# Decoder trunk on one core: side work pauses for eight steps ahead of each wide up-projection group

## The chip, the cores and the metric

The kernel runs on one core of a Trainium2 chip. The metric is the device time of one execution in microseconds; three runs of the kernel before took 2248.45, 2249.08 and 2250.85 us (median 2249.08 us). The profile is of one further execution on the same kind of core.

## What is computed

Two decoder layers over 256 positions of width 2048, in float32. Each layer is a mixer (layer 0: a Mamba-2 scan beside block attention; layer 1: a three-branch sparse attention beside retention), then a convolutional feed-forward network, each followed by a scaled residual and a layer norm. The change lies in the feed-forward part:

```python
D_MODEL, SEQ, DEPTH, FFN_DIM, FFN_CONV = 2048, 256, 2, 5632, 3

def conv_ffn(x, w_up, conv_w, conv_b, w_down):
    a, u = jnp.split(x @ w_up, 2, axis=-1)
    a = causal_depthwise_conv(a, conv_w, conv_b)
    return (jax.nn.silu(a) * u) @ w_down

for layer in range(DEPTH):
    ...
    h = layer_norm(DEEPNORM_ALPHA * h + mix, ln_g[layer, 0], ln_b[layer, 0])
    ffn = conv_ffn(h, ffn_w_up[layer], ffn_conv_w[layer], ffn_conv_b[layer], ffn_w_down[layer])
    h = layer_norm(DEEPNORM_ALPHA * h + ffn, ln_g[layer, 1], ln_b[layer, 1])
```

## The kernel before

**Matmuls.** Every float32 operand is held as a high and a low part, and each product is three matmuls (high by high, high by low, low by high). Weights come from HBM in slabs of mostly 128x1024 numbers (L185, issued by SP into six buffers `wraw`); ScalarE copies out the high part `whi` (L210), VectorE subtracts to get the low part `wlo` (L218), four buffers each. `get` looks three slabs ahead of TensorE.

**Seven products for eight.** Some pairs of 128-row blocks are multiplied with seven block products in place of eight (letters R and N in `PLAN`; P is a plain pair). For these, sums of weight blocks are needed. N forms them when the slabs arrive (`add_up`, L229, into `other` or `sums`). R reads them from DRAM, where they were kept earlier: that is the **side work** of the change. One **cycle** of it (`make`, L231) is two loads of 512 KB into the tile `sums` (L240, issued by POOL), four adds of 128x512 on VectorE (L246), and two stores of 512 KB to DRAM tiles `sumdown...` (L250, POOL). In layer 1 there are 15 cycles for the down projection, all in the one tile `sums`, so a load waits until the stores ahead of it have landed, and the adds wait for the load. `sum_up` (L499) makes the like sums of activations, with VectorE (L509, L513) and a split into high and low parts (L337 on ScalarE, L338 on VectorE).

**The feed-forward part** (`ffn`, L1633) computes the up projection in groups of 256 columns, `a` and `u` in turn (`group_b`, L387: 16 blocks of 128 rows, 64 matmuls), and at a few places one **wide group** of 1024 columns (`group_m`, L517, plan NPNPNPNP): at j=7 in layer 0, at j=4, 8 and 12 in layer 1 (`WIDE_UP`). The last `group_b` ahead of a wide group at j is the one for `u` of j-1 (i odd in the loop). The evacuation of each group multiplies and splits the result into `g` and, from a certain column on, `high`, the input of the down projection.

**Order of the side work.** `Fill` is a list of steps, some of them empty. `group_b` takes one step every second block, so eight in a group. A wide group takes its steps from another list (`aux`) and puts six empty steps ahead of the first when it is done. A cycle of layer 1 spans 14 steps: load, wait 5, add, 1, store, 5 (`CYCLES`, `cycles`). Whatever is left after the last group is run at once (`flush`, L1728). When the last up group of layer 1 starts, the list holds 4 steps, fewer than the eight that the group takes. The emitted instructions then go through a scheduler which sets each engine's order; each engine runs its own in that order.

**Start of the down projection, layer 1.** `finish_rows` (L886) makes four rows for the end of the kernel. It clears `sums` on VectorE (L913), loads rows of `lnrow` into it (L914, by SP), and works them with `rows` on ScalarE (L918, L920) and VectorE (L919, L921), using blocks 0 to 3 of `x` as room. `sum_up` puts the activation sums of the first R pairs into those same blocks of `x`. The first group of the down projection is a `group_m` with the plan PPPPRPRP...: four plain pairs (96 matmuls) come ahead of the first R pair, whose second product reads the first sums in `x`.

Of the kernel before, what the change touches and what calls it, by code (L numbers as in the profile page):

```python
# [321 lines left out]
class Trunk:  # L322
# [1310 lines left out]
    def ffn(self, layer):  # L1633
        nc, x = self.nc, self.x
        with ExitStack() as ctx:
            P = ctx.enter_context(self.tc.tile_pool(name="ffn", bufs=1))
            up, early = ExitStack(), ExitStack()
            wide, first = WIDE_UP[layer], FIRST[layer]
# [57 lines left out]
            def inner(j0):  # L1696
                def turn(j, own, evac):
                    ps = self.ps()
                    for o in range(2):
                        for t in range(2):  # L1700
                            c = 256 * (j - j0) + 128 * o
                            nc.tensor.transpose(ps[:, 256 * o + 128 * t:256 * o + 128 * t + 128], own[t][:, c:c + 128],
                                                self.ident)
                    evac(ps.rearrange("p (a b) -> p a b", a=2), False)

                def go(z):
                    for j in (j0, j0 + 1):
                        for n, f in enumerate((ev_a, ev_u)):
                            self.aux.add(1, lambda j=j, n=n, f=f: turn(j, [z[t][n] for t in range(2)], f(j)))
                return go  # L1710
# [3 lines left out]
            for i, e in enumerate(evacs[3:], 3):  # L1714
                j = i // 2
                if 2 * j == first and i % 2 == 0:
                    assert not self.aux.q and not (double and left)
                    early.close()
                    high = ctx.enter_context(self.tc.tile_pool(name="high", bufs=1)).tile([128, FT - first, 512], F32R, name="high")
                    g = Parts(low, high)  # L1720
                    at = lambda k: g[:, k:k + 2, :]
                if j in wide and i % 2 == 0:
                    assert not self.aux.q
                    self.group_m(x, f"up{layer}", wide.index(j), 0, inner=inner(j))
                    self.fill.q[:0] = [lambda: None] * 6
                elif j not in wide and j - 1 not in wide:
                    self.group_b(x, [e])
            self.fill.flush()  # L1728
            up.close()
# [139 lines left out]
```

## Time and profile before

| what | us |
|---|---|
| runs, median of 3 (lowest to highest) | 2249.08 (2248.45 to 2250.85) |
| the profiled execution: its span, first to last instruction | 2246.8 |
| median of the runs above that span | 2.3 |
| TensorE busy in it | 2235.3 |
| VectorE busy in it | 1831.3 |
| ScalarE busy in it | 1254.0 |
| matmul `ps` at L539 waiting for ScalarE's `whi`, two times | 2.7 |

The span runs from the first to the last instruction of the profiled execution; what a timed run has beyond it lies ahead of and behind the instructions. PE is TensorE, PEld its weight load, DVE is VectorE, ACT is ScalarE, POOL is GpSimd, SP issues most DMAs; a q behind an engine is its sequencer. A row of a timeline gives the start, the duration, the engine, the line and operation, what is written from what, the shape, and in brackets the idle time before it and what ended it. `x2` is a merge of two alike instructions.

### The profile page before, as it was taken

To read this page: it belongs to the slowest core of one execution; us is meant where nothing else is said; L and a number is where in the kernel's file an instruction comes from. 1 tells how busy PE (TensorE), PEld (TensorE's weight loads), DVE (VectorE), ACT (ScalarE), POOL (GpSimd) and SP (SyncE) were. 2 spreads that over 40 slices of the span, in tenths; PEclk is the share of its full clock that TensorE was granted. 3 is DMA by queue.
4 is the path that set the end of the run, shared out by engine and by line. 5 is a ranking of instruction groups with operands and counts; after the bars stand their busy time and mean duration, and the time that the engine had idled before them with its cause. 6 is when DMAs were issued, how large, how long until landed. Compare 5 with 4: busy or idle time off the path is not lost.

```text
span 2246.8 us, 32995 instructions
## 1 busy us (share of the span) xinstructions
PE 2235.3 (99%) x12125; PEld 1920.9 (85%) x12125; DVE 1831.3 (82%) x2795; ACT 1254.0 (56%) x1718; POOL 126.4 (6%) x219
## 2 busy tenths in 40 slices
PE   9999999999999999999999999999999999999998
PEld 9888888888888888888898888888888888888887
DVE  5788688988877778887977777889988887779887
ACT  5555555655555556656645564457555565557563
POOL 0101000110011100000000000000100001100000
PEclk9999999999999999999999999999999999999999
DMA  9854456897788886888668534467876768888884
GB/s 312 292 175 161 158 194 189 274 376 264 238 302 302 296 284 213 292 286 274 211 208 287 188 114 154 152 209 235 290 227 228 255 217 297 300 273 276 276 280 169
DMA packets 158780, 546.33 MB, mean 243 GB/s; under 512 B 17827, under 2 KB 19283, under 8 KB 158483
## 3 DMA queue, kind: packets, MB, share of 16 engines
q1 hardware_dynamic: 132937, 451.41, 60.1%
q0 software_dynamic: 25536, 92.55, 11.8%
q8 instruction: 95, 1.56, 0.3%
q14 instruction: 68, 0.56, 0.1%
q10 hardware_dynamic: 144, 0.26, 0.0%
HBM read 502.19 MB, written 41.96 MB: 242 GB/s over the span
## 4 chain that ended last, share of the span: by engine, by line
PE 96%; DVE 2%; issue 1%; ACT 0%; POOL 0%; DMA 0%; SPq 0%; ACTq 0%; POOLq 0%; DVEq 0%
PE acc L427 51%; PE ps L540 7%; PE ps L541 7%; PE ps L539 7%; PE acc L627 3%; PE acc L629 3%; PE acc L628 3%; PE acc L540 3%; PE acc L541 3%; PE acc L539 3%; PE ps L628 1%; PE ps L627 1%; PE ps L629 1%; PE ps L1161 1%; PE ps L427 1%
## 5 line engine op out<-in xcount | busy, mean ns | idle before, releaser
L210 ACT ACTIVATE whi<-wraw 128x1024 fp32r<-128x1024 f32 (+4 forms) x882 | 875.1, 1002 | 549.6 <-PE acc L427 219.0
L218 DVE TENSOR_TENSOR wlo<-wraw,whi 128x1024 fp32r<-128x1024 f32 (+4 forms) x882 | 1007.5, 1153 | 209.6 <-ACT whi L210 197.6
L427 PE MATMUL acc<-x,whi 128*128 128x512 f32 x3296 | 1032.2, 398 | 0.0
L427 PEld LDWEIGHTS acc<-x,wlo 128*128 128x128 f32 x3296 | 604.0, 188 | 136.5 <-DVE wlo L218 0.3
L427 PE MATMUL acc<-x,wlo 128*128 128x256 f32 x3296 | 633.8, 279 | 0.0
L427 PEld LDWEIGHTS acc<-x,whi 128*128 128x128 f32 x3296 | 510.0, 189 | 9.7 <-issue 1.1
L689 ACT ACTIVATE tmp<-acc 128x512 f32<-128x512 f32 x104 | 62.2, 598 | 167.8 <-PE acc L427 167.7
L246 DVE TENSOR_TENSOR sums<-sums 128x512 f32<-128x512 f32 x140 | 96.2, 687 | 10.5 <-DMA sums<-in_down 9.4
L540 PE MATMUL ps<-wlo,g 128*128 128x512 f32 x260 | 101.3, 390 | 0.0
L541 PE MATMUL ps<-whi,g 128*128 128x512 f32 x260 | 101.2, 389 | 0.0
L539 PE MATMUL ps<-whi,g 128*128 128x512 f32 x260 | 101.2, 389 | 0.0
L539 PE MATMUL ps<-whi,x 128*128 128x512 f32 x244 | 94.0, 390 | 2.7 <-ACT whi L210 2.7
L540 PE MATMUL ps<-wlo,x 128*128 128x512 f32 x244 | 95.5, 391 | 0.1
L541 PE MATMUL ps<-whi,x 128*128 128x512 f32 x244 | 95.0, 389 | 0.0
L627 PE MATMUL acc<-whi,x 128*128 128x344 f32 (+3 forms) x224 | 74.9, 336 | 0.7 <-ACT whi L210 0.7
L628 PE MATMUL acc<-wlo,x 128*128 128x344 f32 (+3 forms) x224 | 74.5, 333 | 0.3 <-DVE wlo L218 0.3
L629 PE MATMUL acc<-whi,x 128*128 128x344 f32 (+3 forms) x224 | 74.3, 332 | 0.0
L1681 DVE SCALAR_TENSOR_TENSOR c<-fpad,prm,c 128x256 f32<-128x256 f32 x176 | 74.2, 479 | 0.0
L210 ACT ACTIVATE whi<-other 128x1024 fp32r<-128x1024 f32 x32 | 33.7, 1055 | 57.7 <-DVE other L229 56.9
L250 POOL DMA_DIRECT2D sumdown<-sums x62 | 33.3, 537 | 570.9 <-DVE sums L246 570.8
L540 PEld LDWEIGHTS ps<-wlo,g 128*128 128x128 f32 x260 | 48.8, 188 | 10.5 <-DVE wlo L218 0.4
L539 PEld LDWEIGHTS ps<-whi,g 128*128 128x128 f32 x260 | 48.8, 188 | 10.3
(458 smaller groups left out, 3141.6 us busy)
## 6 DMA issues: line engine op xcount, KB each, us to landing
wraw<-in_up SPq DMA_DIRECT2D x328, 512.0 KB, 4.8
wraw<-in_down SPq DMA_DIRECT2D x142, 512.0 KB, 4.8
wraw<-in_od_in SPq DMA_DIRECT2D x96, 512.0 KB, 4.2
wraw<-in_ev_in SPq DMA_DIRECT2D x72, 512.0 KB, 4.1
wraw<-sumdown SPq DMA_DIRECT2D x68, 512.0 KB, 4.5
sums<-in_down POOLq DMA_DIRECT2D x62, 512.0 KB, 6.8
sumdown<-sums POOLq DMA_DIRECT2D x62, 512.0 KB, 5.4
wraw<-in_ev_out SPq DMA_DIRECT2D x30, 512.0 KB, 3.9
```

What stands on the lines that cost most here:

```text
L210: a = nc.scalar.activation(hi[:, :n], raw[:, :n], AF.Copy)
L218: b = nc.vector.tensor_tensor(lo[:, :n], raw[:, :n], hi[:, :n].bitcast(F32), op=OP.subtract)
L246: self.tc.keep_in_program_order(nc.vector.tensor_tensor(o, x, y, op=OP.add))
L427: nc.tensor.matmul(acc, wt, mv, start=(k == 0 and i < len(unit)), stop=(k == nk - 1 and i >= len(unit)))
L539: nc.tensor.matmul(o, xh, wh, start=n not in used, stop=False)
L540: nc.tensor.matmul(o, xh, wl, start=False, stop=False)
L541: nc.tensor.matmul(o, xl, wh, start=False, stop=stop)
L627: nc.tensor.matmul(o, xh, wh, start=start, stop=False)
L628: nc.tensor.matmul(o, xh, wl, start=False, stop=False)
L629: nc.tensor.matmul(o, xl, wh, start=False, stop=stop)
L689: nc.scalar.activation(t, a[:, :, 256:], AF.Copy, scale=sign)
L1681: nc.vector.scalar_tensor_tensor(c[:, i, :], pad[:, i, t:t + 256], w[:, t:t + 1], c[:, i, :], op0=OP.mult, op1=OP.add)
```

## The change

In the loop of `ffn`, ahead of the `u` group that stands directly before a wide group, eight empty steps are put at the front of the list. That is the whole group's share, so no step of the side work is taken in it; all later steps come eight steps later. This happens once in layer 0 (j=6) and three times in layer 1 (j=3, 7, 11).

```diff
                 elif j not in wide and j - 1 not in wide:
+                    if j + 1 in wide and i % 2:
+                        self.fill.q[:0] = [lambda: None] * 8
                     self.group_b(x, [e])
             self.fill.flush()
             up.close()
```

No instruction is added or removed. In layer 1 the list is 24 steps longer by the end, so 28 steps are there when the last group starts, and 20 are left to `flush`: the last adds and stores of the second last cycle, and the load, adds and stores of the last. `order` below means the place of instructions on an engine in the built program.

First place, VectorE, the wide group of layer 0 (j=7), from the split of the group ahead of it. `other` holds sums of weight blocks made by `add_up`. Before:

```order
L338 TENSOR_TENSOR g<-u,g 128x2x256
L246 TENSOR_TENSOR sums<-sums 128x512
L218 TENSOR_TENSOR wlo<-wraw,whi 128x1024
L246 TENSOR_TENSOR sums<-sums 128x512
L218 TENSOR_TENSOR wlo<-wraw,whi 128x1024
L246 TENSOR_TENSOR sums<-sums 128x512
L229 TENSOR_TENSOR other<-wraw 128x512
L246 TENSOR_TENSOR sums<-sums 128x512
L229 TENSOR_TENSOR other<-other,wraw 128x512
L229 TENSOR_TENSOR other<-wraw 128x512
L229 TENSOR_TENSOR other<-other,wraw 128x512
```

Now:

```order
L338 TENSOR_TENSOR g<-u,g 128x2x256
L218 TENSOR_TENSOR wlo<-wraw,whi 128x1024 x2
L229 TENSOR_TENSOR other<-wraw 128x512 x2
L229 TENSOR_TENSOR other<-other,wraw 128x512
L218 TENSOR_TENSOR wlo<-wraw,whi 128x1024
L229 TENSOR_TENSOR other<-other,wraw 128x512
L218 TENSOR_TENSOR wlo<-other,whi 128x1024
```

The four adds of a cycle (L246) are gone from here; they stand behind the wide group's evacuation. The wide group at j=4 of layer 1 shows the same.

Second place, VectorE, the wide group at j=12 of layer 1. `fpad` and `u` are the evacuations of the two groups ahead of it. Before:

```order
L246 TENSOR_TENSOR sums<-sums 128x512
L229 TENSOR_TENSOR other<-other,wraw 128x512
L246 TENSOR_TENSOR sums<-sums 128x512
L218 TENSOR_TENSOR wlo<-wraw,whi 128x1024
L246 TENSOR_TENSOR sums<-sums 128x512
L229 TENSOR_TENSOR other<-other,wraw 128x512
L246 TENSOR_TENSOR sums<-sums 128x512
L692 TENSOR_TENSOR fpad_14545<-acc,tmp 128x2x256
L218 TENSOR_TENSOR wlo<-wraw,whi 128x1024
L1681 SCALAR_TENSOR_TENSOR c<-fpad_14545,prm,c 128x256 x4
L229 TENSOR_TENSOR other<-wraw 128x512
```

Now:

```order
L692 TENSOR_TENSOR fpad_14545<-acc,tmp 128x2x256
L218 TENSOR_TENSOR wlo<-wraw,whi 128x1024
L1681 SCALAR_TENSOR_TENSOR c<-fpad_14545,prm,c 128x256 x4
L246 TENSOR_TENSOR sums<-sums 128x512
L218 TENSOR_TENSOR wlo<-wraw,whi 128x1024
L246 TENSOR_TENSOR sums<-sums 128x512
L218 TENSOR_TENSOR wlo<-other,whi 128x1024
L246 TENSOR_TENSOR sums<-sums 128x512 x2
L218 TENSOR_TENSOR wlo<-wraw,whi 128x512
L692 TENSOR_TENSOR u<-acc,tmp 128x512
L1691 TENSOR_TENSOR u<-u,c 128x512
```

The four adds come later than before: they stood ahead of the evacuation `fpad`, and stand now between the splits of the wide group's own first slabs (`wlo` from `wraw`, from `other`, and of 512 columns).

Third place, the end of the up projection in layer 1, VectorE. `high<-u` (L338) is the last split of the up projection. Before:

```order
L338 TENSOR_TENSOR high<-u,high 128x2x256
L218 TENSOR_TENSOR wlo<-wraw,whi 128x1024
L901 MEMSET mean 128x128
L902 MEMSET half 128x1
L903 MEMSET half 128x1
L907 TENSOR_TENSOR sel<-ident 128x1 x2
L913 MEMSET sums 128x2048
L909 TENSOR_TENSOR sel<-sel,ident 128x1
L218 TENSOR_TENSOR wlo<-wraw,whi 128x1024
L910 TENSOR_TENSOR sel<-sel,ident 128x1
```

Now, from the same row on:

```order
L338 TENSOR_TENSOR high<-u,high 128x2x256
L246 TENSOR_TENSOR sums<-sums 128x512
L901 MEMSET mean 128x128
L246 TENSOR_TENSOR sums<-sums 128x512
L902 MEMSET half 128x1
L903 MEMSET half 128x1
L246 TENSOR_TENSOR sums<-sums 128x512
L907 TENSOR_TENSOR sel<-ident 128x1 x2
L246 TENSOR_TENSOR sums<-sums 128x512
L909 TENSOR_TENSOR sel<-sel,ident 128x1
L218 TENSOR_TENSOR wlo<-wraw,whi 128x1024
L910 TENSOR_TENSOR sel<-sel,ident 128x1
```

Some rows later, where before there was no add at all:

```order
L246 TENSOR_TENSOR sums<-sums 128x512
L218 TENSOR_TENSOR wlo<-wraw,whi 128x1024
L246 TENSOR_TENSOR sums<-sums 128x512
L338 TENSOR_TENSOR g<-scratch,g 128x128
L246 TENSOR_TENSOR sums<-sums 128x512
L218 TENSOR_TENSOR wlo<-wraw,whi 128x1024
L246 TENSOR_TENSOR sums<-sums 128x512
L513 TENSOR_TENSOR scratch<-scratch 128x128
L218 TENSOR_TENSOR wlo<-wraw,whi 128x1024
L338 TENSOR_TENSOR g<-scratch,g 128x128
L218 TENSOR_TENSOR wlo<-wraw,whi 128x512
L913 MEMSET sums 128x2048
```

The adds of the second last cycle stand behind the last split, those of the last cycle between the weight splits for the first R pair, and the clearing of `sums` (L913) behind them all.

The same place on SP, the loads of weights for the down projection. Before:

```order
L185 DMA wraw<-sumdown_1_1_14556 128x1024
L185 DMA wraw<-in_down 128x512
L914 DMA sums<-in_lnrow 6x1x2048
L185 DMA wraw<-sumdown_1_0_14555 128x1024
L185 DMA wraw<-in_down 128x1024 x2
```

Now:

```order
L185 DMA wraw<-sumdown_1_0_14555 128x1024
L185 DMA wraw<-in_down 128x1024 x3
L185 DMA wraw<-sumdown_3_1_14558 128x1024
L185 DMA wraw<-in_down 128x512
L914 DMA sums<-in_lnrow 6x1x2048
L185 DMA wraw<-sumdown_3_0_14557 128x1024
```

The load of the rows (L914) has moved back by eight loads of weights. On POOL the order of loads and stores is unchanged. On ScalarE `rows` (L918, L920) stands behind five more pieces of work, and the first split of activation sums into `x` (L337) follows directly on it, where two copies of weights stood between before. On TensorE three matmuls on `g` of the first R pair now stand ahead of the first that reads `x`.

## The prediction

> **What bounds the kernel now.** I read the page's busy times first, then the chain, then the table of waits for PE.
>
> ```profile
> span 2246.8 us, 32995 instructions
> PE 2235.3 (99%) x12125; PEld 1920.9 (85%) x12125; DVE 1831.3 (82%) x2795; ACT 1254.0 (56%) x1718; POOL 126.4 (6%) x219
> PE 96%; DVE 2%; issue 1%; ACT 0%; POOL 0%; DMA 0%; SPq 0%; ACTq 0%; POOLq 0%; DVEq 0%
> L246 DVE TENSOR_TENSOR sums<-sums 128x512 f32<-128x512 f32 x140 | 96.2, 687 | 10.5 <-DMA sums<-in_down 9.4
> PE ps L539 <- ACT whi L210: 2.7, 2, 1.5
> ```
>
> TensorE is busy 2235.3 of 2246.8 us and carries 96% of the chain. No matmul leaves the program, so the change can gain only what TensorE waits, 11.5 us in all, and of this only what waits at the wide groups: L539, two times, 2.7 us, the longer 1.5. Whatever TensorE newly waits for is a loss in full. So there are three questions: do the two waits go, does another come at a wide group, and what becomes of the 24 postponed steps of layer 1.
>
> **The two waits.** The wide group of layer 0, VectorE and then TensorE:
>
> ```profile
> 532.29 0.69 DVE L246 TENSOR_TENSOR sums<-sums 128x512 f32<-128x512 f32 x1
> 532.89 1.22 DVE L218 TENSOR_TENSOR wlo<-wraw,whi 128x1024 fp32r<-128x1024 f32 x1
> 538.77 0.69 DVE L229 TENSOR_TENSOR other<-other,wraw 128x512 f32<-128x512 f32 x1
> 539.58 1.06 ACT L210 ACTIVATE whi<-other 128x1024 fp32r<-128x1024 f32 x1 [6.08 <-DVE other L229]
> 540.69 0.50 PE L539 MATMUL ps<-whi,x 128*128 128x512 f32 x1 [1.22 <-ACT whi L210]
> ```
>
> TensorE waits 1.22 us for `whi`, ScalarE for `other`, which VectorE finishes at 539.46, behind four adds of side work. An add holds VectorE for 0.60 us (from its start at 532.29 to the next at 532.89), so without the four `other` is ready 2.4 us earlier, and the 1.22 us go. The order now has no add there, nor at j=4 of layer 1, where the other wait (1.5 us) is. Taken: **-2.7 us**; bounds 0 and -2.7, as no more is waited. The adds run later, in plain groups. What hides them there is VectorE's idle time and the splits made ahead: of the 140 adds in `sums` only the eight at these two places stand behind a wait of TensorE now. Without that cover a set of four would cost up to 2.4 us.
>
> **The wide group at j=12.** Here the order puts the four adds closer to the group, not further away. Before:
>
> ```profile
> 1783.61 1.67 DVE L1681 SCALAR_TENSOR_TENSOR c<-fpad,prm,c 128x256 f32<-128x256 f32 x4
> 1785.79 1.22 DVE L218 TENSOR_TENSOR wlo<-wraw,whi 128x1024 fp32r<-128x1024 f32 x1
> 1786.93 1.22 DVE L218 TENSOR_TENSOR wlo<-other,whi 128x1024 fp32r<-128x1024 f32 x1
> 1788.06 0.69 DVE L218 TENSOR_TENSOR wlo<-wraw,whi 128x512 fp32r<-128x512 f32 x1
> 1789.66 0.69 DVE L1691 TENSOR_TENSOR u<-u,c 128x512 f32<-128x512 f32 x1
> 1790.27 1.22 DVE L218 TENSOR_TENSOR wlo<-other,whi 128x1024 fp32r<-128x1024 f32 x1
> 1791.74 0.39 PE L540 MATMUL acc<-wlo,part 128*128 128x512 f32 x1
> ```
>
> The second `wlo<-other` ends at 1791.49, and TensorE reads it at 1791.74: 0.25 us to spare. Now VectorE has from 1785.28 on four adds (2.4 us), three splits (1.14, 1.14, 0.60), the evacuation (two of about 0.65) and this split (1.2): 7.8 us, so until 1793.1 to 1793.3, a wait of about **+1.5 us**. Bounds: 0 (if the adds run where VectorE is idle now) and 2.4 (all four).
>
> **The end of the up projection in layer 1.** Of the 24 postponed steps only 4 find room, so two cycles are left over. Before, this place reads, on VectorE, ScalarE and TensorE:
>
> ```profile
> 2013.09 0.68 DVE L338 TENSOR_TENSOR high<-u,high 128x512 fp32r<-128x512 f32 x1
> 2015.76 1.76 DVE L913 MEMSET sums<- 128x2048 f32 x1 [0.37 <-issue]
> 2022.05 1.99 ACT L918 ACTIVATE x<-sums 128x1024 fp32r<-128x1024 f32 x2
> 2023.94 2.18 ACT L920 ACTIVATE x<-x,sel 128x1024 fp32r<-128x1024 f32 x2
> 2026.04 2.48 DVE L921 SCALAR_TENSOR_TENSOR x<-gain,sel,x 128x1024 fp32r<-128x1024 f32 x2
> 2027.92 0.51 ACT L337 ACTIVATE x<-scratch 128x384 fp32r<-128x384 f32 x1
> 2031.30 0.55 DVE L338 TENSOR_TENSOR x<-scratch,x 128x384 fp32r<-128x384 f32 x1
> 2032.01 0.39 PE L541 MATMUL ps<-whi,g 128*128 128x512 f32 x1
> 2032.24 0.39 PE L539 MATMUL ps<-whi,x 128*128 128x512 f32 x1
> ```
>
> This is a chain: `sums` is cleared, rows are loaded into it, worked, and only then may the first activation sums be written into `x`. The low part is ready at 2031.85; TensorE's first read of `x` is at 2032.24, and its third matmul there, the first that needs the low part, comes 0.45 us later. So there is under 1 us to spare. Now the clearing stands behind two sets of adds, and between these lies a way to DRAM and back. Its links are shown by POOL, two cycles earlier, and by the table of DMA issues:
>
> ```profile
> 1983.64 0.54 POOL L250 DMA_DIRECT2D sumdown<-sums  x1 [11.05 <-DVE sums L246]
> 1986.10 0.54 POOL L250 DMA_DIRECT2D sumdown<-sums  x1 [1.93 <-DVE sums L246]
> 1989.38 0.53 POOL L240 DMA_DIRECT2D sums<-in_down  x1 [2.74 <-DMA sumdown<-sums]
> 1992.32 0.53 POOL L240 DMA_DIRECT2D sums<-in_down  x1 [2.41 <-DMA sumdown<-sums]
> sums<-in_down POOLq DMA_DIRECT2D x62, 512.0 KB, 6.8
> sumdown<-sums POOLq DMA_DIRECT2D x62, 512.0 KB, 5.4
> sumev_out<-sums POOLq DMA_DIRECT2D x4, 512.0 KB, 3.7
> wraw<-in_down SPq DMA_DIRECT2D x142, 512.0 KB, 4.8
> out_dram<-r SPq DMA_DIRECT2D x7, 256.0 KB, 2.4
> ```
>
> A store takes 5.4 us to land (3.7 in another stage), a load 6.8 (4.8 for weights of the same size), each load waits for its store, and POOL adds about 0.5 us from the last add to the store and 0.3 from landing to load. The adds that stood at 1981.9 are now those of the fourth last cycle, so the load at 1992.32 is the third last's. I follow the second halves:
>
> - third last cycle: load in at 1999.1, its second add waits for this; three adds with a split between end near 2002.4; stored 2008.3; second last load in at 2015.4.
> - second last: its adds stand behind the split at 2013.77; the second waits until 2015.4; done 2017.6; stored 2023.5; last load in at 2030.6.
> - last: the second to fourth add, with two splits between, 3.6 us: 2034.2; stored 2040.1, or 2038.4 at 3.7 us. I take the latter: SP can issue no more weights then, since `wraw` is full as long as these splits wait, and its next transfer but a few is the held L914.
> - clearing 1.8: 2040.2; 4.5 from its end to L918 as before (2017.52 to 2022.05): 2044.7; `rows` 4.1, split 0.5: high part at 2049.3. The low part has two L919 and two L921 ahead on VectorE, 6.5 us from L918's start, and 0.55: 2051.7. TensorE can do four matmuls on the high part first (0.23 each): it goes on at about 2050.8.
>
> Without the wait TensorE would be there at 2032.9 (three matmuls on `g` now go first, 0.68 us). So it stands for **+18 us**. Waits that come sooner, for weights whose splits are held behind the adds, lie within this. Bounds: at the lowest, all loads in time and the shortest rows: 2013.8, adds 2.8, store 0.5 + 3.7, load 0.3 + 4.8, adds and splits 3.6, store 4.2, clearing 1.8, the rows' load 2.4 (the shortest in the table), then 6.1 (7.0 to the low part, less the four matmuls), 2044.0, so +11; at the highest, stores and loads 2 us longer in each of the last three links, +24. What is queued behind the held instructions: on VectorE weight splits, which TensorE wants no sooner; on SP L914 holds later weight loads to 2041, and the gain rows behind it to 2050, but the next slab that TensorE lacks is wanted only after the R pair and another plain pair, over 10 us after it resumes. After the wait VectorE has some 2.5 us of split sums ahead of the next weights; TensorE has 15 matmuls left in the R pair, 3.4 us, so this is hidden, or costs 1 us.
>
> In layer 0 the list ends with one empty step, so the one pause there costs nothing at the end.
>
> **The clock after the wait.** At its start the kernel shows slow matmuls after idleness:
>
> ```profile
> 1.05:4.20 3.15, 3.14 (x14) 1.00 0.73 217
> 4.30:5.10 0.80, 0.73 (x7) 1.00 0.93 339
> ```
>
> (The columns are the length, TensorE's busy time and count, granted clock, share and rate of DMA.) The same 128-column matmul takes 0.22 us each in the first 3.1 us, 0.10 to 0.11 after, though the clock column says 1.00 in both. After the waits of 1.22 and 1.5 us nothing like it is seen. A wait of 18 us is nearer to the start of the kernel: 3.1 us at half speed lose 1.5. Taken: **+1.5**, bounds 0 and 1.6. The Trainium skill, "TensorE: Matmul & The Clock Gate", Part 1, says that TensorE's clock falls to half after an idle window of about 3.4 us and comes back after one busy window; by that rule the sum is the one with this term, without it 1.5 us less. That is the rule that speaks against the change, and the trace's first 4.2 us agree with it; no row here shows it in mid-kernel.
>
> **The sum.** -2.7 + 1.5 + 18 + 1.5 = +18.3 us: a span of 2265.1, and with the 2.3 us by which the median of the runs exceeds the span, 2267.4 us.
>
> **Rivals.**
> - *The tail is hidden, and the change does what its words say.* Then only the two waits go: 2246.4. It needs the first sums in `x` by 2032.9, that is, a chain longer by no more than about 1 us than before. Against it: store, load and store of the last two cycles all come after 2013.8 in VectorE's and POOL's order, 11 us even by the shortest row. It would hold only if the clearing of `sums` did not wait for the stores. 4%.
> - *The pauses miss.* The adds still meet the wide groups, at j=12 by the order itself, and each costs its 1.2 to 1.5 us somewhere else: the gain of 2.7 is eaten, and with the tail the time is 2271. As the whole, without the tail, it would be within 0.2%: 3%.
> - *The short tail.* All transfers run as the shortest rows do, because the held weights leave the DMA engines idle: +11 and no slow clock: 2249.1 + 11 - 2.7 + 1.5 = 2259. 20%.
> - *The long tail.* Held splits and SP's held queue add up, and TensorE, once it resumes, waits again for weights: +24 + 1.6 + 3: 2276. 13%.
> - My forecast, between 2261 and 2273: 60%.
>
> **How the numbers follow.** 2267.4 us. The range from 2256 to 2274 takes in the short tail and the forecast and leaves out the two cases without a tail and the far end of the long one. Faster or slower by over 0.2% means 4.5 us, about what a measurement of this kernel tells from none: faster 4%, same 3%, slower 93%.
>
> **What would show it.** In the profile after: no wait of L539 for `whi` at the wide groups of j=7 and j=4; one of 1 to 2 us at j=12; one wait of 15 to 20 us, in one or two pieces, at the first R pair of the down projection, released by the split into `x` (L337 or L338); stores (L250) that land near 2040 with L913 directly behind; 14 or so matmuls at double time after it. The forecast is wrong if the clearing comes before 2030, or if TensorE has no gap over 5 us there.

## Result and profile after

The changed kernel takes 2265.22 us (median of 5 runs, 2262.90 to 2266.32), the kernel before 2249.08 us (5 runs, 2248.45 to 2250.85): a ratio of 1.0071, 95% interval 1.0060 to 1.0082. The forecast was 2267.4 us, range 2256 to 2274. The profiled execution of the changed kernel took 2265.63 us, with a span of 2263.8 us, 17.0 us more than before.

From the page of the changed kernel, the span, the busy times, the chain and two groups:

```profile
span 2263.8 us, 32992 instructions
PE 2238.4 (99%) x12125; PEld 1921.8 (85%) x12125; DVE 1832.0 (81%) x2795; ACT 1254.6 (55%) x1718; POOL 126.7 (6%) x219
PE 94%; DMA 2%; DVE 2%; issue 1%; ACT 0%; POOL 0%; SPq 0%; DVEq 0%; ACTq 0%; POOLq 0%
L246 DVE TENSOR_TENSOR sums<-sums 128x512 f32<-128x512 f32 x140 | 96.3, 688 | 20.9 <-DMA sums<-in_down 19.7
L539 PE MATMUL ps<-whi,x 128*128 128x512 f32 x244 | 94.8, 391 | 14.9 <-ACT x L337 14.9
```

The same number of matmuls and adds. TensorE is busy 3.1 us longer for the same work, the chain has 2% of DMA in it where it had none, and the one wait of 14.9 us is released by the write into `x`. PE's table of waits (total, times, longest), its first two rows:

```profile
PE ps L539 <- ACT x L337: 14.9, 1, 14.9
PE ps L540 <- DVE wlo L218: 1.2, 2, 1.0
```

The row for `whi` at L539, 2.7 us before, is gone. The end of the up projection of layer 1, from the timelines of POOL, VectorE, ScalarE and TensorE (in this order in time):

```profile
2014.82 0.54 POOL L250 DMA_DIRECT2D sumdown<-sums  x1 [7.83 <-DVE half L903]
2020.07 0.54 POOL L240 DMA_DIRECT2D sums<-in_down  x1 [0.84 <-DMA sumdown<-sums]
2025.03 0.69 DVE L246 TENSOR_TENSOR sums<-sums 128x512 f32<-128x512 f32 x1 [3.23 <-DMA sums<-in_down]
2027.45 0.69 DVE L246 TENSOR_TENSOR sums<-sums 128x512 f32<-128x512 f32 x1 [0.60 <-DMA sums<-in_down]
2030.00 0.69 DVE L246 TENSOR_TENSOR sums<-sums 128x512 f32<-128x512 f32 x1
2031.25 0.54 POOL L250 DMA_DIRECT2D sumdown<-sums  x1 [2.27 <-DVE scratch L513]
2032.08 0.51 PE L540 MATMUL ps<-wlo,g 128*128 128x512 f32 x1 [0.96 <-DVE wlo L218]
2037.51 1.76 DVE L913 MEMSET sums<- 128x2048 f32 x1 [4.68 <-DMA sumdown<-sums]
2043.13 2.00 ACT L918 ACTIVATE x<-sums 128x1024 fp32r<-128x1024 f32 x2 [10.43 <-DMA sums<-in_lnrow]
2047.12 0.51 ACT L337 ACTIVATE x<-scratch 128x384 fp32r<-128x384 f32 x1
2047.68 0.80 PE L539 MATMUL ps<-whi,x 128*128 128x512 f32 x1 [14.87 <-ACT x L337]
```

It reads as one chain: store, load, adds held for the load (3.23 and 0.60 us of VectorE waiting), store (2031.25), clearing held for that store (4.68 us), rows, first sums into `x`, TensorE. Clearing starts 21.75 us later than before (2015.76).

Laying the two traces over each other matmul by matmul gives the lag of the changed kernel (when a matmul starts there, less when it starts before; a negative lag is a lead), and with it the account of the 17.0 us. The lag is nearly level over long stretches, with steps between them: +0.44 up to the wide group of layer 0 and -0.89 behind it, a step of -1.33; -0.69 ahead of j=4 and -1.90 behind it, -1.21; level at -1.90 from there to 2029, past j=8 and j=12; +14.76 at the matmul that resumes, +16.66; +16.84 nine matmuls on, +2.08. What is left, +0.8, is the 0.44 at the start of the kernel (in the traces of the ten other kernels it lies between -0.15 and +0.4) and two pieces of 0.2 us. At j=4 the wait of 1.50 us is gone, but a shorter one is new:

```profile
1623.11 0.50 PE L540 MATMUL ps<-wlo,x 128*128 128x512 f32 x1 [0.28 <-DVE wlo L218]
```

### The profile page after: what moved, and what is told of

Its sections match the earlier page's. It is cut to its first block, busy times and chain, and to the rows that moved or that the text cites. A ratio compares the mean times of both kernels' runs of the same rounds, so it can differ in the third digit from the quotient of the medians.

```text
span 2263.8 us, 32992 instructions
## 1 busy us (share of the span) xinstructions
PE 2238.4 (99%) x12125; PEld 1921.8 (85%) x12125; DVE 1832.0 (81%) x2795; ACT 1254.6 (55%) x1718; POOL 126.7 (6%) x219
## 4 chain that ended last, share of the span: by engine, by line
PE 94%; DMA 2%; DVE 2%; issue 1%; ACT 0%; POOL 0%; SPq 0%; DVEq 0%; ACTq 0%; POOLq 0%
PE acc L427 49%; PE ps L540 7%; PE ps L539 7%; PE ps L541 7%; PE acc L627 3%; PE acc L629 3%; PE acc L628 3%; PE acc L540 3%; PE acc L541 3%; PE acc L539 3%; PE ps L629 1%; PE ps L628 1%; PE ps L627 1%; DMA sums<-in_down 1%; DMA sumdown<-sums 1%
## 5 line engine op out<-in xcount | busy, mean ns | idle before, releaser
L246 DVE TENSOR_TENSOR sums<-sums 128x512 f32<-128x512 f32 x140 | 96.3, 688 | 20.9 <-DMA sums<-in_down 19.7
L539 PE MATMUL ps<-whi,x 128*128 128x512 f32 x244 | 94.8, 391 | 14.9 <-ACT x L337 14.9
L539 PE MATMUL ps<-whi,g 128*128 128x512 f32 x260 | 101.2, 389 | 0.0
L539 PEld LDWEIGHTS ps<-whi,x 128*128 128x128 f32 x244 | 45.9, 188 | 25.0 <-ACT x L337 15.3
```

The source lines that it names most:

```text
L246: self.tc.keep_in_program_order(nc.vector.tensor_tensor(o, x, y, op=OP.add))
L539: nc.tensor.matmul(o, xh, wh, start=n not in used, stop=False)
```

## The experiments

Ten further kernels were timed against the kernel before, 4 to 11 times each. Medians of the kernel before in these series: 2248.89 to 2249.14 us. The four that settle the cause come first.

**Pause in layer 0 alone.**

```diff
-                    if j + 1 in wide and i % 2:
+                    if layer == 0 and j + 1 in wide and i % 2:
```

> The pause is made in layer 0 alone; layer 1 has none. Theory (the whole loss is the chain through `sums` at the end of layer 1's up projection): no gap of TensorE over 1 us at the first R pair, `sums` cleared near 2016 us as before, the wait for `whi` at j=7 gone and the one at j=4 of layer 1 still there: 2249.1 - 1.3 = 2247.8 us. Rival (a pause costs by itself, because its adds meet other work in the plain groups): each of the four pauses costs some 4 us, so about 2253 us with the loss spread over the up projection of layer 0.

Measured: 2247.62 us (2247.06 to 2248.22, 11 runs), ratio 0.9993 (0.9985 to 1.0002). In PE's table of waits the first row is

```profile
PE ps L539 <- ACT whi L210: 1.5, 1, 1.5
```

so the wait at j=7 is gone, that at j=4 stays, and there is no gap at the first R pair. A pause by itself costs nothing here.

**The tail alone, in the kernel before.** No pause anywhere, but 24 more empty steps behind the wide group at j=12 of layer 1:

```diff
-                    self.fill.q[:0] = [lambda: None] * 6
+                    self.fill.q[:0] = [lambda: None] * (30 if layer == 1 and j == 12 else 6)
```

> The kernel before, with 24 empty steps more behind the wide group j=12 of layer 1 and no pause ahead of any group: the same steps are left over at the end, and nothing else is moved ahead of j=4 of layer 1 or in layer 0. Theory: the two waits for `whi` stay as before and the tail comes whole (16.4 us of waiting, about 2.1 us of slow matmuls): 2249.1 + 18.5 = 2267.6 us, `sums` cleared near 2037 us. Rival (the pauses ahead of the groups cost): about 2249 us.

Measured: 2267.62 us (2267.08 to 2268.01, 4 runs), ratio 1.0082 (1.0068 to 1.0096). PE's table of waits:

```profile
PE ps L539 <- ACT x L337: 14.8, 1, 14.8
PE ps L539 <- ACT whi L210: 2.7, 2, 1.5
```

Both the old waits and the new one are there: the loss comes from two cycles left over at the end, whether the steps are lost ahead of the wide groups or behind the last of them.

**Clearing taken off `sums`.** In the changed kernel the rows are loaded into `gain` in place of `sums` (which `finish_rows` calls `self.bias`), and their low part is made in `scratch`, which is passed to it:

```diff
-        raw, low = self.bias, self.gain
+        raw, low = self.gain, scratch
...
-            h, l, z, o = (v[:, c:c + 1024] for v in (parts[0], low, raw, self.gb))
+            (h, z, o), l = (v[:, c:c + 1024] for v in (parts[0], raw, self.gb)), low
```

> The changed kernel, but the rows at the end are loaded into `gain` and their low part is made in `scratch`, so that clearing (L913) no longer waits for the last store out of `sums`; the two left-over cycles are done as in the changed kernel. Theory (the round trips to DRAM through `sums` hold the clearing): L913 comes before the last adds, the rows' transfer is done while they wait, and the first sums go into `x` behind the last adds (2030.7 us) and some splits, near 2038 in place of 2047.7: a wait of 4 to 8 us, 2254 to 2259 us. Rival (what holds TensorE is the adds and the weight splits held behind them in VectorE's order, not the clearing): the wait stays at 14 to 17 us, 2263 to 2266 us.

Measured: 2256.83 us (2255.12 to 2258.46, 5 runs), ratio 1.0033 (1.0021 to 1.0046). From the timelines:

```profile
2014.41 1.76 DVE L913 MEMSET gain<- 128x2048 f32 x1 [0.38 <-issue]
2033.17 0.50 PE L540 MATMUL ps<-wlo,g 128*128 128x512 f32 x1 [3.31 <-DVE wlo L218]
2038.25 0.79 PE L539 MATMUL ps<-whi,x 128*128 128x512 f32 x1 [4.35 <-ACT x L337]
```

Clearing comes 23 us sooner than in the changed kernel, and the wait for `x` falls from 14.87 to 4.35 us. But 3.31 us now show at `wlo`: a weight split that stands on VectorE behind the last adds, which wait 2.25 and 1.68 us for their loads, and behind work on the rows (L919, L921) that lies between. Two things were in the tail, and the longer one hid the shorter.

**The same with the low part made in place**, so that `scratch` isn't shared either:

```diff
-        raw, low = self.bias, self.gain
+        raw, low = self.gain, self.gain
```

> The changed kernel with the rows loaded into `gain` and their low part made in place there, so that neither `sums` nor `scratch` ties the rows to other work; both left-over cycles as in the changed kernel. Theory (of the gap that stayed with the rows in `gain` and `scratch`, 3.3 us is the weight split held behind the last adds, the rest mostly the shared `scratch`): the 3.3 us stay, the wait for `x` falls from 4.3 to 1 to 3 us, 2252 to 2255.5 us. Rival (nothing of it is due to `scratch`): 2256.8 us as before this edit.

Measured: 2255.41 us (2254.71 to 2256.62, 7 runs), ratio 1.0031 (1.0019 to 1.0042). The two large rows became

```profile
2033.25 0.52 PE L540 MATMUL ps<-wlo,g 128*128 128x512 f32 x1 [3.67 <-DVE wlo L218]
2037.55 0.79 PE L539 MATMUL ps<-whi,x 128*128 128x512 f32 x1 [1.93 <-ACT x L337]
```

As expected the wait for `x` lost 2.4 us, while the waiting for `wlo` grew by 0.5 (3.67 us, and a second piece of 0.19). The median is 1.4 us lower, at the upper end of the expected range, but the two intervals overlap, so the runs alone don't show a gain. Of the 15.8 us of waiting in the tail (14.87 and 0.96) some 10 thus hang on clearing; of the 5.8 us that stay, 3.9 are weight splits that stand behind the adds and the rows' work in VectorE's order. The rows' work alone doesn't make them late: with one left-over cycle, whose adds wait for nothing, the same edit leaves a gap of 0.2 us (further down).

**Catching up by shorter cycles.** All four pauses, cycles of 12 steps in layer 1:

```diff
-CYCLES = ((6, 10, 13), (0, 0, 14))
+CYCLES = ((6, 10, 13), (0, 0, 12))
```

> All four pauses stay, but a cycle of layer 1 takes 12 steps in place of 14, so that the 15 cycles need 30 steps less and the list is empty before the last group. Theory: both waits for `whi` gone and no tail: 2249.1 - 3 = 2246 us, TensorE resumes at the first R pair without a gap over 1 us. Rival (the pauses cost by themselves): near 2265 us, as the pauses are the same. Second rival (12 steps are too few for a store and a load, so the adds wait for loads and hold the weight splits): gaps of 0.5 to 1 us at the groups of layer 1, 2250 to 2258 us.

Measured: 2251.39 us (2248.72 to 2252.83, 11 runs), ratio 1.0009 (0.9999 to 1.0018). The tail is gone, as the theory says, but so is the gain; the second rival was nearest. Its largest loss is one that none of the three named, at the wide group j=4 (POOL, then VectorE, then TensorE):

```profile
1599.10 0.54 POOL L240 DMA_DIRECT2D sums<-in_down  x1 [0.69 <-DMA sumdown<-sums]
1599.63 1.07 POOL L869 DMA_DIRECT2D room<-in_lnrow  x2
1608.28 0.69 DVE L873 SCALAR_TENSOR_TENSOR r<-r,room 128x512 f32<-128x512 f32 x1 [0.43 <-DMA room<-in_lnrow]
1609.82 0.69 DVE L877 SCALAR_TENSOR_TENSOR r<-room,r 128x512 f32<-128x512 f32 x1 [0.84 <-DMA room<-in_lnrow]
1615.97 0.75 PE L540 MATMUL acc<-wlo,part 128*128 128x512 f32 x1 [1.30 <-DVE wlo L218]
```

In the new phase POOL issues the two loads for the residual (`room`, L869) behind both loads of a cycle. In the kernel before they went ahead of them:

```profile
1599.58 0.55 POOL L869 DMA_DIRECT2D room<-in_lnrow  x1 [1.20 <-DVE r L873]
1601.32 0.56 POOL L869 DMA_DIRECT2D room<-in_lnrow  x1 [1.19 <-DVE r L877]
1601.87 0.53 POOL L240 DMA_DIRECT2D sums<-in_down  x1
```

They go out at nearly the same time (1599.63), but take 9.1 us to land (median of the two) where they took 7.0. VectorE waits for them, and the split that TensorE needs comes 1.30 us late, right behind a wait of 0.39 us. That it is the loads ahead of them that slow them is argued from this order and wasn't tested. Later, at 1937.69, TensorE waits 1.67 us for a split behind two adds that wait 5.93 and 1.90 us for their loads: there 12 steps are too few for store and load.

**One pause in layer 1** (ahead of j=4; layer 0 as in the change), nothing else:

```diff
-                    if j + 1 in wide and i % 2:
+                    if j + 1 in (wide[:1] if layer else wide) and i % 2:
```

> Of the three pauses of layer 1 only the one ahead of its first wide group (j=4) stays, beside that of layer 0: 8 steps are postponed, 4 of them have no room, and one set of four adds stands behind the last split of the up projection in place of two. Theory (a chain through `sums`, one round trip and not two): adds done near 2016, stored near 2020 to 2022, cleared near 2022 to 2024 against 2017.5 before, so TensorE waits 4 to 6 us at the first R pair, and both waits for `whi` are gone: 2249.1 - 3.3 + 5 + about 0.7 of slow matmuls = 2251.5 us. Rival (it is the steps flushed at once that cost, in proportion: 4 of 20): a wait of 3 us or less, 2249 us. Rival (any left-over cycle costs the whole tail): 2262 us or more.

Measured: 2248.64 us (2247.22 to 2253.59, 11 runs), ratio 1.0002 (0.9993 to 1.0011). The expected wait of 5 us isn't there in the profiled run, of 2247.35 us, the second fastest of the eleven:

```profile
2011.34 0.68 DVE L246 TENSOR_TENSOR sums<-sums 128x512 f32<-128x512 f32 x1
2014.78 0.54 POOL L250 DMA_DIRECT2D sumdown<-sums  x1 [1.20 <-DVE sel L909]
2018.79 1.76 DVE L913 MEMSET sums<- 128x2048 f32 x1 [0.43 <-issue]
2032.32 0.50 PE L541 MATMUL ps<-whi,x 128*128 128x512 f32 x1 [0.46 <-DVE x L338]
```

The adds wait for nothing, since the load of the only left-over cycle was in before them, and clearing, though 3 us later than before, is early enough: 0.46 us of waiting. What costs is the second left-over cycle, whose load must wait for the first one's store. The first rival's numbers fit (3 us or less, 2249 us), the theory's don't; yet 4 of 20 steps in proportion would be 3.2 us of the 15.8, and 0.46 is far less.

The scatter of these runs up to 2253.6 us, far wider than before's, can't be placed by this profile; a later kernel gives a hint.

**Later cycles shorter, one pause in layer 1:** the kernel just described, and one step less in the last eight steps between cycles:

```diff
-                fill.add(period - 4 - wait)
+                fill.add(period - 4 - wait - (period == 14 and i >= len(made) - 9))
```

> The same two pauses, and the last eight steps between cycles of layer 1 are one shorter (13 steps in place of 14 for the later cycles), so that the eight postponed steps are caught up late in the layer, where no residual work is left; on VectorE the end of the up projection is in the order of before. Theory: no tail, both waits gone, and nothing of what made period 12 wait: 2249.1 - 3.3 = 2245.8 us. Rival (13 steps are too few for store and load, as with 12): one to three gaps of 0.5 to 2 us in the later groups, 2247 to 2250 us.

Measured: 2247.35 us (2246.15 to 2249.28, 11 runs), ratio 0.9993 (0.9984 to 1.0002): no tail, both waits gone, 0.49 us of new waiting at j=12. That is above the theory and near the lower end of the rival's range.

**One pause in layer 1 and the rows off `sums`,** first with the low part in `scratch`, then in place (edits as above):

> The same two pauses with the rows at the end loaded into `gain` and their low part made in `scratch`, so that clearing does not wait for `sums`. Theory: the one left-over cycle is harmless, since nothing at the first R pair waits for its stores: no gap over 1.5 us there, 2246 to 2248 us. Rival (the adds and the splits held behind them): a gap of 3 us or more as in the single pause with `sums`, 2250 us or more.

Measured: 2254.16 us (2252.45 to 2256.09, 11 runs), ratio 1.0023 (1.0014 to 1.0032), so worse than with `sums`. ScalarE shows why:

```profile
2035.10 0.52 ACT L337 ACTIVATE x<-scratch 128x384 fp32r<-128x384 f32 x1 [0.28 <-DVE scratch L513]
```

The first sums are made in `scratch` and now queue for it behind the rows; TensorE waits 3.4 us at L539. The edit brought its own wait. The rival's numbers fit, but its reason, the adds and the splits behind them, isn't what the next kernel shows.

> Pauses ahead of the wide group of layer 0 and of j=4 in layer 1 alone, and the rows loaded into `gain` with their low part made in place. Theory (the gap of 3.4 us with the low part in `scratch` came from the first sums that queue for `scratch` behind the rows): no gap over 1.5 us at the first R pair, 2246 to 2248.5 us, and none of the scatter up to 2253.6 us that the single left-over cycle showed with `sums`. Rival (adds and splits behind the last `high` cost by themselves): a gap of 3 us, 2252 to 2254 us.

Measured: 2248.59 us (2247.47 to 2252.25, 11 runs), ratio 1.0 (0.9991 to 1.0009). The gap at the first R pair is down to 0.2 us, so it was `scratch`; the time lies just above the expected range. The scatter stays, so it doesn't come from clearing alone. This profile, of a run of 2250.09 us, has a wait elsewhere, at j=12:

```profile
1786.98 0.69 DVE L246 TENSOR_TENSOR sums<-sums 128x512 f32<-128x512 f32 x1 [2.88 <-DMA sums<-in_down]
1792.12 0.50 PE L540 MATMUL acc<-wlo,part 128*128 128x512 f32 x1 [1.30 <-DVE wlo L218]
```

With 8 steps postponed and no pause there, an add inside the wide group waits for a load, by 2.88 us here and by 0.92 us in the profile of the kernel with `sums`, where TensorE did not wait. How late the load lands may well make the scatter; that it makes all of it isn't shown.

**Pauses at j=4 and j=12, nearly all cycles 13 steps:** the list of pauses is `wide[::2]`, and the shorter step begins at the second gap between cycles (`len(made) - 14`).

> Pauses ahead of j=4 and j=12 of layer 1 (and of j=7 in layer 0), and 13 steps in place of 14 for all but the first cycles of layer 1: 16 steps are postponed and 13 caught up, so that the end of the up projection stands on VectorE as before. Theory: both waits for `whi` gone, no tail, and no adds ahead of the last split of j=12, which cost 0.5 to 1.3 us where that pause was missing: 2249 - 3.3 + 0 to 0.5 = 2245.7 to 2246.2 us, below the 2247.35 us of the version with one pause in layer 1. Rival (shorter cycles meet the residual work around j=4 as period 12 did, or the adds wait for loads in the plain groups): 2248 to 2251 us.

Measured: 2247.71 us (2246.62 to 2249.34, 11 runs), ratio 0.9994 (0.9985 to 1.0003). Its profile, of its fastest run, has none of the waits in dispute and a span of 2244.8 us, but the median is no better than that of one pause, and lies between what theory and rival forecast. Three versions thus stand 1.2 to 1.6 us under the kernel before of their series, two more (one pause in layer 1, with the rows in `sums` or in place) 0.3 and 0.4 us, and every interval takes in 1: a gain from the pauses without a tail is likely and small, but no single version shows it clear of noise.

## Why the prediction was right, step by step

- **The two waits, -2.7.** Right in place and kind, and nearly in size: -1.33 and -1.21 between the level stretches, 2.5 us. Neither matmul waits for `whi` any more, but at j=4 TensorE now waits 0.28 us for the next low part, so not all that was waited could be gained. Putting no pause in layer 1 brought one of the two waits back.
- **The wide group at j=12, +1.5.** Wrong; it cost nothing. The step that failed is the sum of 7.8 us from 1785.28 on (four adds, three splits, the evacuation and this split). I put the four adds on top of the work of before, at before's time, but they only moved from ahead of `fpad` to behind it: ahead of the split that was in question there is as much work as ever. VectorE and TensorE of the changed kernel:

```profile
1779.48 1.67 DVE L1681 SCALAR_TENSOR_TENSOR c<-fpad,prm,c 128x256 f32<-128x256 f32 x4
1781.06 0.69 DVE L246 TENSOR_TENSOR sums<-sums 128x512 f32<-128x512 f32 x1
1784.54 1.41 DVE L246 TENSOR_TENSOR sums<-sums 128x512 f32<-128x512 f32 x2
1787.04 0.69 DVE L692 TENSOR_TENSOR u<-acc,tmp 128x512 f32<-128x512 f32 x1 [0.48 <-ACT tmp L689]
1788.37 1.22 DVE L218 TENSOR_TENSOR wlo<-other,whi 128x1024 fp32r<-128x1024 f32 x1
1789.85 0.39 PE L540 MATMUL acc<-wlo,part 128*128 128x512 f32 x1
```

  `c<-fpad` starts 4.13 us earlier than before (1783.61), TensorE's read only 1.89 us: those 2.24 us are the adds that no longer stand ahead. The split ends at 1789.59, 0.26 us ahead of the read, as before (0.25). VectorE even stood still ahead of the evacuation `u`, 0.48 us for ScalarE's `tmp` (0.18 before), so the adds had room to spare. The wait does exist where an add has to wait for its load: 0.49 and 1.30 us in two of the experiments.
- **The tail, +18.** Right in mechanism and place, 16.7 in size. Clearing was put at 2038.4 and came at 2037.51, so close by luck, as two errors work against each other: the last adds end 3.5 us sooner than worked out (2030.69 against 2034.2), since the adds of the second last cycle were done 1.6 us sooner and their store took 3.8 us from its issue to the load it released (2016.29 to 2020.07), where 5.7 was taken; that load was no quicker than the median. And the last store took 6.8 us from the last add to the clearing, where 4.2 was taken. From the end of clearing to L918 it took 3.9 us, not 4.5. And TensorE resumed 4.55 us behind L918, not 6.1: it goes on when the high part is in `x`, and at half speed the low part catches up with it. That makes 3.1 us; 1.9 us go the other way, as the kernel came to this place that much sooner, while the chain was laid on the times of before.
- **The clock, +1.5 (at most 1.6).** Right in kind, 2.1 in size; the upper bound was wrong, since 3.1 us, the slow stretch at the start of the kernel, was taken for the length of such a stretch. The windows of the changed kernel ahead of, in and behind it (length, busy time and count of PE, PEld, DVE, ACT and POOL, granted clock, DMA share, GB/s):

```profile
2044.00:2047.60 3.60, 0.00 (x0) 0.00 (x0) 3.38 (x3) 3.60 (x5) 0.00 (x0) 0.50 0.00 0
2047.60:2052.20 4.60, 4.52 (x11) 3.34 (x12) 4.46 (x11) 1.71 (x4) 0.00 (x0) 0.52 0.67 187
2052.20:2056.80 4.60, 4.60 (x22) 3.77 (x21) 4.60 (x5) 3.40 (x5) 0.00 (x0) 1.00 0.62 196
```

  Eleven matmuls in 4.6 us at a clock of 0.52, where 22 go at full speed behind it; the slow part lasts some 4.3 us. The tail alone cost 2.05 us in the same way.
- **The sum.** -2.54 + 0 + 16.66 + 2.08 + 0.8 (the start and two small pieces, for which the forecast had no term) = 17.0, where 18.3 was forecast. The median is 0.4 us under the profiled execution, and this 1.8 us above its span, where 2.3 was taken. The errors partly cancel: the forecast is 2.2 us off, the terms by up to 1.5.
- **The rival "the tail is hidden",** which "would hold only if the clearing of `sums` did not wait for the stores", was the wrong condition by itself: with clearing set free, two left-over cycles still cost 5.8 us of waiting (3.67, 0.19 and 1.93), since the adds hold the splits of weights and the first sums behind them. In its profile it nearly holds with one left-over cycle (0.46 us), and then it needs no edit of the clearing.

## What to carry to other kernels

Postponing side work is free only as long as its list still ends in time: count the steps that are postponed against those that the list has to spare, and what the last of them releases. Here a remainder was priced by its round trips through a shared tile and not by its steps: one left-over cycle whose load was already in cost 0.46 us of waiting in its profile, two cost 15.8. When work is moved within an engine's order, take it off the place it leaves before adding it where it comes to.

## What the runs showed of the hardware

The granted clock halves after less idleness than I had thought. In the kernel with cycles of 12 steps TensorE waited 0.39 and, half a microsecond later, 1.30 us; behind it the clock stood at 0.52 for 3.5 us, and the stretch cost 1.5 us more. After the single wait of 1.50 us in the kernel before nothing fell (nor after that of 1.22 us), nor after the single wait of 1.67 us at 1937.69 in that same execution with 12 steps. The windows behind the two waits and behind the one of 1.67 us, with the columns as above:

```profile
1615.90:1619.40 3.50, 3.43 (x8) 2.76 (x9) 3.50 (x6) 1.43 (x2) 0.00 (x0) 0.52 0.19 27
1937.60:1941.00 3.40, 3.31 (x19) 2.96 (x20) 3.40 (x5) 0.99 (x2) 1.07 (x2) 1.00 0.93 305
```

and that behind the single wait of 1.50 us in the kernel before:

```profile
1623.60:1627.00 3.40, 3.31 (x14) 2.74 (x15) 3.33 (x4) 3.28 (x5) 0.53 (x1) 1.00 0.89 254
```

The length of the idleness alone hardly decides between 1.67 and 1.69 us. The mean clock in windows of 1 us places the changes: down at 1616.04 and up at 1619.45 in this kernel (3.41 us), 2034.31 and 2041.13 with the rows in `gain` and `scratch` (6.82), 2034.96 and 2052.03 in the changed kernel (17.07); three further kernels with such a fall give 3.42, 6.83 and 17.07. These are one, two and five times 3.41 us, as if the clock changed only at the ends of stretches of that length that run on through the kernel. Both pieces, 1.69 us, lie in the stretch that ends at 1616.04. Counted on from there, an end falls near 1936.9, so by this estimate the wait of 1.67 us was cut into 0.9 and 0.8. It would also explain why the slow part outlasted the forecast's 3.1 us: in the changed kernel TensorE came back at 2047.68, 4.35 us ahead of the end at which the clock rose.

The Trainium skill, "TensorE: Matmul & The Clock Gate", Part 1, has the clock fall after an idle window of about 3.4 us and come back after a busy one of that length. The length and the way back agree (3.41 us here, some 4.3 us in the changed kernel); the fall doesn't, as 1.69 us of idleness in two pieces were enough in this run. How much of a stretch has to be idle was not tried.
